# Order of emission around the block products of a ConvFFN: a norm's broadcast inside a product, weight sums a step ahead of their splits, the sample operand kept in SBUF, a second load queue

## The chip, the cores and the metric

The kernel runs on one core of one Trainium2 chip. The metric is the device time of one execution in microseconds (us). The core has a matrix engine, TensorE (PE, with a weight load, PEld, that overlaps its matmuls), VectorE (DVE), ScalarE (ACT), GpSimd (POOL) and SyncE (SP); each works its own list of instructions in order, and they wait for each other through semaphores. Transfers are issued from an engine's list (here SP's and POOL's) and carried out by the core's 16 DMA engines.

## The reference

One inference step of one layer: a mixer (retention and gated linear attention heads, with one input and one output projection), and behind it a gated ConvFFN with a causal convolution of width 3, for 1024 prompt frames and 64 sample frames of a running stream (1088 columns in all). Everything is float32. The part that the change touches is this:

```python
x = x + g1 * jnp.einsum('bte,ed->btd', mix, w_out)
h2 = _rmsnorm(x, g_norm_ffn) * (1.0 + sc2) + sh2
a, up = jnp.split(jnp.einsum('btd,df->btf', h2, w_ffn_in), 2, axis=-1)   # 1024 -> 2 x 2816
buf = jnp.concatenate([conv0.astype(a.dtype), a], axis=1)
conv = conv_b + conv_w[0] * buf[:, 0:T]
for j in range(1, CONV_W):
    conv = conv + conv_w[j] * buf[:, j:j + T]
y = jax.nn.silu(conv) * up
x = x + g2 * jnp.einsum('btf,fd->btd', y, w_ffn_out)                     # 2816 -> 1024
...
y_prompt = _rmsnorm(xp, g_final)                                         # and y_sample alike
```

The last two columns of `a` per row (`buf[:, T:]`) are outputs too (the caches).

## The kernel before

**Number format.** A float32 product is made of three passes over reduced floats: each operand is split ("cut") into a high part `hi` (a cast on ACT) and a low part `lo` (source minus `hi`, on DVE), and PE adds hi*hi, hi*lo and lo*hi. So each operand costs ACT one pass, DVE one.

**Norm ahead of the FFN (L1456, L1560 to 1608).** The output projection runs over three token groups `c` (384, 384, 320 columns) and eight row blocks `m`; each (c, m) ends with a residual addition into `hf[m]` (tiles named `ab`, or `cv` for m = 6, 7) and an addition of its squares to `sqs`. `norm2(c, sqs)` then has two halves: PE sums `sqs` over partitions (`ones`), DVE makes the reciprocal root in a dozen small operations (`na`, `nr`); PE broadcasts it over the partitions (`ident,nr`), and DVE multiplies `hf` by it and the modulation. The third group's norm is spread over the first products of FFN-in.

**FFN-in (L1488 to 1860).** The matrix product is made with seven block products p = 1..7 in place of eight (a Strassen scheme on halves of the inner dimension and halves of the columns), for 22 blocks `q` of 128 rows: 11 pairs of a convolution row and its gate row. A product is 24 matmuls of 128x272 (`product`, L1701). Its two operands are a sum or difference of weight blocks (made by `prep_in`, L1508, with its inner `need` for the sums `ws` and `raw`, and cut into a slot of three `hi` and three `lo` tiles, L1503), and a sum or difference of halves of the normed columns (`X`, made once by `operand` and `sums_b`). `prep_to(n)` has the first n products' weights made; within the loop (L1854) it runs LA = 4 products ahead. `evict_in` (L1714) takes a product out of PSUM, mostly by additions on DVE; convolution, gate and the sums of the gated rows for FFN-out's own block products (`y_sums`, L1670) are queued in `aux` and run within a budget of each step. The gated rows go to DRAM (`d_y`) from POOL's queue, the sample columns of each to `d_ys` (L1664). The first products' order (q = 0 and (1,1)) is written out by hand (L1780 to 1815).

**FFN-out (L1821 to 2246).** The list `osteps` has the steps of the seven products: "M" p=1 for 11 row blocks, "A" p=2 and p=4 in pairs of blocks, M 6, A 3, M 7, A 3, A 5 and "B" 5. For a step, weights come in through `rw` buffers (5) and gated rows through `ry` (3, M steps) or `rb` (3, A and B steps; `load_b`, L1998, and the split into `ba`, 11 buffers). All these loads are on SP's queue. A step has its operands cut three steps ahead (`prep_out`). The sample columns come back by 22 loads of 32 KB through SP (`sp_group`, L1904) and are cut into `sp`. The finished rows are added to the residual `x3` (16 loads from `d_x2`, L2141) by DVE (`add_to`); `caches` (L2102) transposes the cache rows, copies them on DVE into `cs` and stores them. Some intermediate weight sums go to DRAM (`d_e`) from POOL.

**Final norm.** `final_first` (L2084) norms the first 512 columns beside the last products. For the rest, `late_turn` transposes each 128-row group in two halves (one early, one at the end), ACT squares them with a sum (`square`), and `finish` (L2039) makes the factor and multiplies each half by it and the gain `gbc` into `yt`, with one store per group.

## Time and profile before

| | us |
|---|---|
| median of 3 runs | 1524.76 (1523.64 to 1531.74) |
| profiled execution | 1522.7 |
| its span, first to last instruction | 1520.9 |
| PE busy | 1372.5 (90%) |
| DVE busy | 1091.0 (72%) |
| ACT busy | 627.5 (41%) |
| POOL busy | 296.3 (19%) |

The mean granted clock of PE is 0.973 of full speed. The shares are means over stages with different limits, so the table by stretches further down is read first: it gives for each stretch the time that each engine was busy in it, with the number of instructions, then the granted clock, the DMA engines' share and the rate in GB/s. In a timeline a row is a run of equal instructions: its start, its time, engine, line and operation (out<-in), and in brackets how long the engine stood idle before it and who released it. L234, L239 and L91 are helpers through which most instructions go, so tiles' names tell them apart. SPq is SyncE issuing transfers.

### The profile page before, as it was taken

How to read it: one execution, taken by the hardware profiler on the slowest of the kernel's cores; microseconds unless marked ns; L12 is line 12 of the kernel's file. 1: busy time of each engine (PE TensorE's matmuls, PEld its weight loads, DVE VectorE, ACT ScalarE, POOL GpSimd, SP SyncE). 2: the span in 40 equal slices, each digit the busy share in tenths (PEclk: the TensorE clock that was granted, in tenths of full speed). 3: DMA queues.
4: the chain of work that ended last, by engine and by line, in shares of the span. 5: the costliest groups of instructions: out<-in, count | busy, mean ns of one | idle time of the engine just before them, and what ended most of it. 6: DMA issues, size and time to landing. Idle time of an engine off the chain costs nothing.

```text
span 1520.9 us, 23779 instructions
## 1 busy us (share of the span) xinstructions
PE 1372.5 (90%) x9082; PEld 1270.4 (84%) x9082; DVE 1091.0 (72%) x1992; ACT 627.5 (41%) x1253; POOL 296.3 (19%) x394
## 2 busy tenths in 40 slices
PE   5999888989989899898689999999999978899995
PEld 3778778879879898898589999999999956687874
DVE  6647878966885888667787777777777745667766
ACT  5645344432333224455454434434444433343342
POOL 3335434424332443211001111101000100000000
PEclk9999999999999999999899999999999989999998
DMA  8420101132223222564113323332233259653522
GB/s 258 151 68 15 56 19 58 42 96 85 87 87 99 77 82 68 171 196 151 33 28 106 101 85 106 106 106 63 74 105 106 97 184 334 215 164 115 178 74 111
DMA packets 165913, 165.75 MB, mean 109 GB/s; under 512 B 13289, under 2 KB 131399, under 8 KB 165799
## 3 DMA queue, kind: packets, MB, share of 16 engines
q1 hardware_dynamic: 157159, 135.99, 29.1%
q0 software_dynamic: 8640, 28.25, 4.7%
q8 instruction: 71, 1.16, 0.3%
q14 instruction: 43, 0.35, 0.1%
HBM read 130.67 MB, written 33.53 MB: 108 GB/s over the span
## 4 chain that ended last, share of the span: by engine, by line
PE 47%; DVE 27%; ACT 9%; DMA 6%; issue 6%; SPq 0%; POOL 0%; DVEq 0%; ACTq 0%; POOLq 0%
PE dX L234 17%; PE mm L234 11%; PE dA L234 6%; PE al L234 4%; PE mn L234 3%; DVE lo L91 3%; PE o L234 2%; DMA raw<-in_w_ffn_in_dram 2%; DVE ab L91 2%; ACT hi L91 2%; DVE qbd L91 2%; ACT cv L91 2%; DVE cv L91 2%; DVE acc L91 2%; DVE raw L91 2%
## 5 line engine op out<-in xcount | busy, mean ns | idle before, releaser
L234 PE MATMUL dX<-X,lo 128*128 128x272 f32 x1344 | 182.0, 291 | 15.5 <-ACT X L91 7.0
L234 PEld LDWEIGHTS dX<-X,lo 128*128 128x128 f32 x1344 | 174.3, 190 | 18.8 <-DVE ab L91 8.2
L234 PE MATMUL dX<-X,hi 128*128 128x272 f32 x1296 | 174.2, 290 | 6.3 <-DVE ab L91 5.6
L234 PEld LDWEIGHTS dX<-X,hi 128*128 128x128 f32 x1296 | 168.5, 190 | 6.7 <-issue 5.7
L234 PE MATMUL mm<-act_hi,hi 128*128 128x384 f32 (+1 forms) x480 | 169.7, 354 | 0.3 <-DVE mix L91 0.2
L234 PE MATMUL mm<-act_lo,hi 128*128 128x384 f32 (+1 forms) x480 | 158.0, 329 | 0.1
L234 PE MATMUL mm<-act_hi,lo 128*128 128x384 f32 (+1 forms) x480 | 157.7, 329 | 0.0
L91 ACT CAST hi<-raw 128x512 fp32r<-128x512 f32 (+1 forms) x122 | 97.1, 798 | 71.3 <-DVE raw L91 60.5
L234 PE MATMUL al<-ba,hi 128*128 128x512 f32 x396 | 102.2, 400 | 7.0 <-DVE x L91 7.0
L234 PE MATMUL mn<-lo,hi 128*128 128x512 f32 x396 | 99.8, 406 | 8.4 <-ACT lo L91 4.6
L234 PEld LDWEIGHTS mn<-lo,hi 128*128 128x128 f32 x396 | 76.2, 195 | 29.6 <-ACT lo L91 7.2
L91 DVE SCALAR_TENSOR_TENSOR cv<-ab,cw,cv 128x1088 f32<-128x1088 f32 x44 | 59.3, 1348 | 48.9 <-ACT cv L91 48.9
L234 PEld LDWEIGHTS mm<-act_hi,hi 128*128 128x128 f32 x480 | 91.3, 190 | 1.9 <-DVE mix L91 0.5
L234 PEld LDWEIGHTS mm<-act_lo,hi 128*128 128x128 f32 x480 | 91.2, 190 | 0.7 <-POOL act_lo L91 0.3
L234 PEld LDWEIGHTS al<-ba,hi 128*128 128x128 f32 x396 | 71.9, 191 | 22.8 <-DVE x L91 8.3
L234 PEld LDWEIGHTS mm<-act_hi,lo 128*128 128x128 f32 x480 | 90.8, 189 | 0.0
L234 PE MATMUL mm<-hi,act_hi 128*128 128x256 f32 x288 | 87.7, 304 | 0.2 <-ACT hi L91 0.2
L234 PE MATMUL mm<-lo,act_hi 128*128 128x256 f32 x288 | 82.3, 286 | 4.1 <-DVE lo L91 4.1
L234 PE MATMUL mm<-hi,act_lo 128*128 128x256 f32 x288 | 82.1, 285 | 0.0
L91 POOL TENSOR_TENSOR acc<-acc,prod 128x512 f32<-128x512 f32 x42 | 64.9, 1546 | 81.3 <-ACT prod L91 80.4
L91 DVE TENSOR_TENSOR lo<-raw,hi 128x1024 fp32r<-128x1024 f32 x49 | 64.0, 1308 | 13.7 <-ACT hi L91 13.6
L234 PE MATMUL dX<-act_hi,hi 128*128 128x384 f32 (+1 forms) x192 | 66.4, 346 | 8.0 <-DVE ab L91 7.2
(334 smaller groups left out, 3096.2 us busy)
## 6 DMA issues: line engine op xcount, KB each, us to landing
raw<-in_w_ffn_in_dram SPq DMA_DIRECT2D x44, 512.0 KB, 3.8
raw<-in_w_ada_dram SPq DMA_DIRECT2D x32, 512.0 KB, 4.0
raw<-in_w_in_dram SPq DMA_DIRECT2D x28, 512.0 KB, 3.8
raw<-in_w_out_dram SPq DMA_DIRECT2D x24, 512.0 KB, 4.0
d_y<-cv POOLq DMA_DIRECT2D x22, 512.0 KB, 4.7
rb<-d_y SPq DMA_DIRECT2D x44, 256.0 KB, 2.9
rw<-in_w_ffn_out_dram SPq DMA_DIRECT2D x41, 256.0 KB, 3.0
wa<-in_w_ada_dram SPq DMA_DIRECT2D x16, 512.0 KB, 4.9
```

Source lines behind the costliest of these rows:

```text
L91: return call(*args, **kw)
L234: T.matmul(out, lhsT, rhs, start=start, stop=stop, skip_group_check=more)
```

## The change

1. *Sample operand.* Three of the `hf` tiles (m = 3, 4, 5) move from the `ab` tiles to a pool `spp` of their own, whose three tiles are used again, once the norm is done, for the sample operand `sp` of the whole FFN. The gate writes the high half of its 64 sample columns there by an ACT copy, and DVE the low half with the next `y_sums`. `d_ys`, its 22 stores and 22 loads, and `sp_group` are gone.
2. *Entry.* The sums of q = 0 are made behind `prep_to(4)`, during the last steps of the output projection; product (0,2) is cut in two halves, with the rest of the third group's norm between; the hand order of operands, evictions and preparations is another, and the look-ahead LA is 5.
3. *FFN-out.* `rb` loads are issued by POOL; `d_e` stores go a step later; the sums of a step's weights are made a step ahead of their cut (`sum_out`); `rw` has four buffers; the PSUM tiles `mn` take other banks.
4. *Final norm.* The early halves are multiplied by the gain before the factor is known (`late_gain`), and by the factor on ACT; DVE makes the late halves alone. One small operation of the factor is gone, by a scale in the squares. The pairs of transposes in `final_first` come without a step between.

The diff, cut to its core:

```diff
-        return abp.tile([P, 2 + T2], F32, tag=tag, name=tag, bufs={"ab0": 2, "ab": 6, "cv": 2}[tag])
+        return abp.tile([P, 2 + T2], F32, tag=tag, name=tag, bufs={"ab0": 2, "ab": 3, "cv": 2}[tag])
-    hf = [ab_tile("ab" if k < 6 else "cv") for k in range(KD)]
+    hf = [ab_tile("ab" if k < 3 else "cv") if k < 3 or k > 5 else
+          spp.tile([P, T2], F32, tag="sp", name="hf", bufs=3) for k in range(KD)]
...
                 prep_to(4)
+                for n in range(1, 5):
+                    need_in(0, n)
...
-            nc.gpsimd.dma_start(out=d_ys[f], in_=cv[:, SEQ:T2])
-        aux.append(("D", fn, 1.3))
+        def hi():
+            S.copy(out=spart(f)[:, 0:SMP], in_=cvt[q // 2, n][:, SEQ:T2])
+        def lo():
+            V.tensor_tensor(out=spart(f)[:, SMP:P], in0=cvt[q // 2, n][:, SEQ:T2],
+                            in1=spart(f)[:, 0:SMP].bitcast(F32), op=ALU.subtract)
+        aux.extend([("D", fn, 1.3), ("A", hi, 0.0)])
+        small_lo.append(lo)
...
+    LA = 5
     evict_in(0, 1)
-    product(0, 2)
-    for _ in gen:
-        pass
+    prep_to(6)
+    product(0, 2, 0, 2)
+    all_of(gen)
+    product(0, 2, 2, 4)
     product(1, 1)
-    prep_to(6)
-    LA = 4
-    sums_b(1, 2 * CW - HT, HT)
-    all_of(operand(5, 0, 1 - 1, xbp))
-    sums_b(3, 2 * CW - HT, HT)
+    sums_b(1, edge, HT)
+    all_of(operand(5, 0, 0, xbp))
     product(0, 5)
     all_of(operand(3, 1, 1, xbp))
     evict_in(0, 5)
-    prep_to(8)
+    product(0, 3)
+    sums_b(3, edge, HT)
     sums_b(2, 0, HT)
-    product(0, 3)
     all_of(operand(6, 1, 1, xbp))
     evict_in(0, 3)
-    prep_to(9)
+    prep_to(7)
     product(0, 6)
     all_of(operand(7, 0, 1, xbp))
     evict_in(0, 6)
+    prep_to(8)
+    product(0, 7)
     sums_b(4, 0, HT)
-    product(0, 7)
...
-    pmn = ctx.enter_context(tc.tile_pool(name="pmn", bufs=4, space=PSUM, reuse_waits="tile"))
     pal = ctx.enter_context(tc.tile_pool(name="pal", bufs=3, space=PSUM, reuse_waits="tile"))
     psm = ctx.enter_context(tc.tile_pool(name="psm", bufs=1, space=PSUM, reuse_waits="tile"))
+    pmn = ctx.enter_context(tc.tile_pool(name="pmn", bufs=4, space=PSUM, reuse_waits="tile"))
-    ftag = {"rw": 5, "ry": 3, "rb": 3}
+    ftag = {"rw": 4, "ry": 3, "rb": 3}
-                nc.gpsimd.dma_start(out=d, in_=w)
+                stores.append((d, w))
...
-        nc.sync.dma_start(out=t, in_=d_y[i][:, YI[p]])
+        nc.gpsimd.dma_start(out=t, in_=d_y[i][:, YI[p]])
...
-    sp_group(0, 8)
-            sp_group(8, 3)
-            sp_group(11, 6)
-            sp_group(17, 5)
+        elif n + 3 < len(osteps):
+            sum_out(n + 3)
+        for d, w in late_stores:
+            nc.gpsimd.dma_start(out=d, in_=w)
+        late_stores[:] = stores
+        stores[:] = []
...
+            for j in {0: (), 1: (0,), 2: (1, 2, 3)}[n - len(osteps) + 3]:
+                late_gain(j)
...
-    for _ in finish(late, P, 4, tsq, lambda j: y_prompt[0, (4 + j) * P:(5 + j) * P, :]):
-        pass
+    rs = rsqrt(vv, 4, "n4")
+    for j in range(4):
+        r, yt = rs[:, j:j + 1], yts[j]
+        early_, (pt, cols) = cols_of(0)(yt), late[j][1]
+        S.activation(out=early_, in_=early_, func=AF.Copy, scale=r)
+        V.scalar_tensor_tensor(out=cols(yt), in0=pt, scalar=r, in1=cols(gbc), op0=ALU.mult,
+                               op1=ALU.mult)
+        nc.sync.dma_start(out=y_prompt[0, (4 + j) * P:(5 + j) * P, :], in_=yt)
```

PE at the entry to FFN-in, before: `dA<-X` and `dX<-X` are products of 24 matmuls, `ones,sqs` the sum of squares, `ident,nr` the broadcast, L239 transposes of the convolution's taps.

```order
L234 MATMUL dA<-X_7458,hi 128x272 x24
L234 MATMUL dX<-ones,sqs 128x1 x3
L239 MATMUL dX<-ident,ab_7578 128x88
L239 MATMUL dX<-ident,ab_7578 128x44
L234 MATMUL dA<-X_7515,lo 128x272 x24
L234 MATMUL dX<-ident,nr 128x128 x3
L234 MATMUL dA<-X_7458,hi 128x272 x24
L234 MATMUL dX<-X_7803,lo 128x272 x24
```

The same place on PE after the change:

```order
L234 MATMUL dA<-X_7439,hi 128x272 x24
L234 MATMUL dX<-ones,sqs 128x1 x3
L239 MATMUL dX<-ident,ab_7559 128x88
L239 MATMUL dX<-ident,ab_7559 128x44
L234 MATMUL dA<-X_7496,lo 128x272 x12
L234 MATMUL dX<-ident,nr 128x128 x3
L234 MATMUL dA<-X_7496,lo 128x272 x12
L234 MATMUL dA<-X_7439,hi 128x272 x24
```

The broadcast has moved from behind the second product to its middle.

DVE at the same place, before, from the last residual addition of the projection (`cv<-dX,G`) and around it: `raw` and `ws` are weight sums, `hi`, `lo` the low parts of cuts, `ab<-ab 128x224` and `128x320` differences of the columns; between the two halves stand the dozen small operations of the factor and the normed operands.

```order
L91 TENSOR_TENSOR lo<-ws,lo 128x512
L91 TENSOR_TENSOR ab<-ab 128x224 x6
L91 TENSOR_TENSOR ab<-cv,ab 128x224 x2
L91 SCALAR_TENSOR_TENSOR cv<-dX,G_129,cv 128x256
...
L91 SCALAR_TENSOR_TENSOR cv<-cv,A_127,dX 128x64
L91 TENSOR_TENSOR raw<-raw 128x512
L91 TENSOR_TENSOR raw<-ws,raw 128x512
L91 TENSOR_TENSOR raw<-raw 128x512
L91 TENSOR_TENSOR hi<-raw,hi 128x512
L91 TENSOR_TENSOR lo<-raw,lo 128x512
L91 TENSOR_TENSOR ab<-ab 128x320 x4
```

DVE there after the change:

```order
L91 TENSOR_TENSOR lo<-ws,lo 128x512
L91 TENSOR_TENSOR raw<-raw 128x512
L91 TENSOR_TENSOR raw<-ws,raw 128x512
L91 TENSOR_TENSOR raw<-raw 128x512
L91 TENSOR_TENSOR ab<-ab 128x224 x3
...
L91 SCALAR_TENSOR_TENSOR cv<-dX,G_129,cv 128x256
...
L91 SCALAR_TENSOR_TENSOR nr<-na,nr 128x3
L91 TENSOR_TENSOR hi<-raw,hi 128x512
L91 TENSOR_TENSOR lo<-raw,lo 128x512
L91 SCALAR_TENSOR_TENSOR ab<-ab,A_127,dX 128x256
```

The three sums stand ahead of the last residual addition, and the two subtractions of the cut ahead of the normed operands.

SP's queue at the exit of FFN-in, before, behind the last 14 sample loads (the last of them in the first row): `C` and `ry` are weights and gated rows of FFN-out, `x_...` residual rows.

```order
L1907 DMA rb<-d_ys_6486 128x64
L2136 DMA C_12847<-in_w_ffn_out_dram 128x512 x3
L1934 DMA C_12847<-in_w_ffn_out_dram 128x512
L1938 DMA ry<-d_y_6459 128x512
L2001 DMA rb<-d_y_6454 128x512
L2001 DMA rb<-d_y_6455 128x512
L2001 DMA rb<-d_y_6456 128x512
L2108 DMA out_dram<-cs 44x128
L2141 DMA x_0_0_12849<-d_x_6453 128x512
```

The same place on SP after the change:

```order
L1946 DMA C_12852<-in_w_ffn_out_dram 128x512
L1950 DMA ry<-d_y_6458 128x512
L2159 DMA C_12852<-in_w_ffn_out_dram 128x512 x3
L1946 DMA C_12852<-in_w_ffn_out_dram 128x512
L1950 DMA ry<-d_y_6459 128x512
L2125 DMA out_dram<-cs 44x128
L2164 DMA x_0_0_12854<-d_x_6453 128x512
```

The sample loads and the `rb` loads have left SP's queue; the `rb` loads stand on POOL's, behind its last store of `d_y`, and later between the `d_e` stores.

## Rows read from the trace of the kernel before

**Rows 1.** Table by stretches; columns in its first row (x: instructions; PEclk: granted clock).
```profile
core 0: us, PE busy (x) PEld busy (x) DVE busy (x) ACT busy (x) POOL busy (x), PEclk, DMA share, GB/s
705.00:776.00 71.00, 47.71 (x287) 45.30 (x287) 57.22 (x118) 36.06 (x75) 4.78 (x12) 0.83 0.14 43
776.00:1216.00 440.00, 433.99 (x3443) 431.79 (x3442) 324.53 (x440) 187.40 (x313) 38.99 (x120) 1.00 0.29 93
1225.20:1282.20 57.00, 42.73 (x158) 31.19 (x158) 25.52 (x41) 18.73 (x33) 3.46 (x7) 0.88 0.85 286
1282.20:1319.60 37.40, 36.89 (x179) 28.94 (x178) 24.04 (x39) 11.29 (x20) 5.93 (x11) 1.00 0.67 223
...
1396.00:1504.50 108.50, 105.85 (x478) 85.06 (x479) 76.96 (x143) 41.15 (x83) 0.00 (x0) 1.00 0.38 124
1504.50:1520.90 16.40, 2.56 (x20) 1.85 (x18) 8.96 (x23) 3.11 (x10) 0.00 (x0) 0.67 0.32 128
```

**Rows 2.** Waits of PE, 705 to 776; total, times, longest.
```profile
PE dX L234 <- ACT X L91: 7.0, 1, 7.0
```

**Rows 3.** Timeline of PE at the entry; start, time, run of instructions.
```profile
731.97 4.72 PE L234 MATMUL dA<-X,lo 128*128 128x272 f32 x24 [0.94 <-ACT ab L91]
...
778.99 3.17 PE L234 MATMUL dX<-X,lo 128*128 128x272 f32 x24
```

**Rows 4.** Timeline of DVE at the entry.
```profile
737.40 3.59 DVE L91 SCALAR_TENSOR_TENSOR ab<-ab,A,dX 128x256 f32<-128x256 f32 x12 [4.50 <-PE dX L234]
...
742.07 0.69 DVE L91 TENSOR_TENSOR raw<-raw 128x512 f32<-128x512 f32 x1
...
746.10 1.69 DVE L91 TENSOR_TENSOR ab<-ab 128x320 f32<-128x320 f32 x4
```

**Rows 5.** Waits of PE, 790 to 1216, the products.
```profile
PE dX L234 <- DVE ab L91: 6.0, 10, 1.5
```

**Rows 6.** Timeline of SP's queue at the exit; L1907 sample loads, L2141 residual loads.
```profile
1226.82 13.47 SPq L1907 DMA_DIRECT2D rb<-d_ys  x14
...
1250.79 1.75 SPq L2141 DMA_DIRECT2D x<-d_x  x4
```

**Rows 7.** Timeline of PE at the exit.
```profile
1238.10 1.22 PE L234 MATMUL sm<-hi,sp 128*128 128x512 f32 x2 [7.74 <-DVE sp L91]
1239.12 5.09 PE L234 MATMUL mn<-lo,hi 128*128 128x512 f32 x12
...
1244.53 3.01 PE L234 MATMUL mn<-lo,hi 128*128 128x512 f32 x12
```

**Rows 8.** Transfers of the stretch 1255 to 1282: packets, bytes, mean rate.
```profile
DMA packets 6583, 9.75 MB, mean 361 GB/s; under 512 B 1612, under 2 KB 2533, under 8 KB 6581
```

**Rows 9.** Timeline of POOL at the exit: its last store of FFN-in.
```profile
1232.26 0.54 POOL L1687 DMA_DIRECT2D d_y<-ab  x1
```

**Rows 10.** Transfers issued 1282 to 1320: count, KB each, median us to landing.
```profile
rb<-d_y SPq DMA_DIRECT2D x9, 256.0 KB, 4.9
d_e<-rw POOLq DMA_DIRECT2D x9, 256.0 KB, 3.4
```

**Rows 11.** Timeline of PE between the A steps of p=2 and p=4.
```profile
1325.54 1.65 PE L234 MATMUL al<-ba,hi 128*128 128x512 f32 x3 [5.96 <-DVE x L91]
```

**Rows 12.** Timeline of DVE there.
```profile
1324.74 1.40 DVE L91 SCALAR_TENSOR_TENSOR x<-al,G,x 128x512 f32<-128x512 f32 x2
```

**Rows 13.** Tile rb: idle time of its engines before it; us, times.
```profile
  DMA rb<-d_y: 20.3, 13
```

**Rows 14.** Timeline of PE in the last products; L239 transposes rows.
```profile
1498.00 0.66 PE L239 MATMUL al<-ident,x 128*128 128x128 f32 x4 [1.74 <-DVE yt L91]
```

**Rows 15.** Tile yt: least/median/most ns, first to last start; DMA landing.
```profile
L2052 SPq DMA_DIRECT2D out_dram<-yt x9: 332/333/511, 1393.3 to 1517.0; - x9
...
L91 DVE SCALAR_TENSOR_TENSOR yt<-mn,n4r,gbc x4: 741/741/742, 1512.1 to 1516.2; 128x512 f32<-128x512 f32 x4
...
DMA to landing us min/median/max: 2.6/2.6/2.6
```

More of the change, by code (lines that the diff above doesn't have):

```diff
@@ L1378, in stream_step_kernel @@
     d_y = [scr.tile([P, 7, 512], F32, name=f"d_y{i}") for i in range(KF)]
-    d_ys = [scr.tile([P, SMP], F32, name=f"d_ys{f}") for f in range(NF)]
     d_e = {}
@@ L1506, in combo_slot, with need_in @@
         return wp.tile(shape, F32R, tag=tag, name=tag, bufs=3)
+    def need_in(q, n):
+        if (q, n) in sums:
+            return 0.0
+        (a11, a12), (a21, a22) = ((raws[q, i][:, 0:4], raws[q, i][:, 4:8]) for i in range(2))
+        cost = 0.7
+        if n == 1:
+            s = sums[q, 1] = fw.tile([P, 4, P], F32, tag="ws", name="ws", bufs=2)
+            plus(s, a21, a22)
+            return cost
+        if n == 3:
+            cost += need_in(q, 1)
+            sub(a21, a11, a21)
+        elif n == 2:
+            cost += need_in(q, 3)
+            sub(a11, sums[q, 1], a11)
+        else:
+            cost += need_in(q, 2)
+            sub(a12, a12, a11)
+        sums[q, n] = True
+        return cost
     def prep_in(q, p):
@@ L1699, in run_aux, with product @@
                 last_d[0] = now[0]
-    def product(q, p):
+    def product(q, p, k0=0, k1=4):
         grp = {1: "A", 2: "A", 6: "B", 7: "B", 5: "C", 3: "C", 4: "D"}[p]
         first = p in (1, 6, 5, 4)
-        if first:
+        if first and k0 == 0:
             held[q, grp] = pair("dA" if grp == "A" else "dX")
         o = held[q, grp]
-        t, x = combos.pop((q, p)), X[p]
-        for k in range(4):
+        t, x = combos[q, p], X[p]
+        for k in range(k0, k1):
             for a, b in ((0, 0), (0, 1), (1, 0)):
@@ L1778, in cached_taps, with all_of @@
         plus(e01[:, 0], e01[:, 0], et)
+    def all_of(g):
+        for _ in g:
+            pass
+    LA = 5
+    edge = 2 * CW - HT
     gen = norm2(2, sqs)
@@ L1953, in load_to, with sum_out @@
             o_load[0] += 1
+    def sum_out(n):
+        st = osteps[n]
+        kind, p = st[:2]
+        if kind == "M" and p == 6:
+            w = rw[n] = ft("rw")
+            sub(w, C2[:, st[2]], C1[:, st[2]])
+        elif kind == "M" and p == 7:
+            sub(rw[n], C1[:, st[2]], rw[n])
+        elif kind == "A" and p == 3:
+            u, i, k = st[2:]
+            w = rw[n][:, 0:k]
+            sub(w, w, C2[:, i:i + k, u * 256:u * 256 + 256])
+    stores = []
     def prep_out(n):
```

95 lines of the change are left out of this document (38 added, 57 removed).

## Prediction

> **What bounds the kernel now.** I read the table by stretches first [rows 1]: for each stretch of the span it has TensorE's (PE) busy time, the granted clock and the DMA engines' share. The change touches nothing before 705 us (the mixer and the first two token groups of the norm), so only later stretches count. They are limited by different things. From 776 to 1216 us, the block products of FFN-in, PE is busy 433.99 of 440.00 us at a clock of 1.00: only 6 us are there to be had. The entry to that stretch (705 to 776) has PE busy 47.71 of 71.00, with DVE (VectorE) busy 57.22: DVE holds it up. The exit (1225.2 to 1282.2) has PE busy 42.73 of 57.00 and the DMA share at 0.85: transfers hold it up. From 1396 to 1504.5 PE is busy again (105.85 of 108.50), and the tail of 16.40 us is DVE and the last stores. So the change can win in the gaps: about 23 us at the entry, 6 in the products, 14 at the exit, 6 at one stall, 3 in the last products, and part of the 16 of the tail.
>
> **The change part by part.** The sums below are made against the profiled execution, 1522.7 us (span 1520.9); the median of the runs stands 2.1 us above it.
>
> *Entry.* The chain of waits here: PE runs product (0,2) whole, 4.72 us from 731.97, and broadcasts the norm factors only behind it [rows 3]. DVE, which had the factors ready, waits 4.50 us for that broadcast, makes the normed operands (737.40 on), then three weight sums and a pair of splits (742.07 to 746.10, 4.0 us), and only then the differences that feed operand 5, for which PE waits 7.0 us [rows 2, 4]. The change cuts product (0,2) in two halves with the broadcast between them, so the broadcast comes 12 matmuls (half of 4.72, so about 2.4 us) earlier; and it puts the three sums ahead of the norm's last residual add and the splits' two subtractions just before the normed operands. The sums (3 x 0.72 = 2.2 us) therefore lie on the path to the statistics and push them back 2.2; the earlier broadcast gives 2.4 back. So the normed operands start where they did, and the 4.0 us behind them are gone from the path. Against this, the look-ahead of 5 puts one more sum and one more split (0.69 each, 1.4 us) into DVE's queue ahead of an eviction, and the sums for operands 3 and 2 now stand behind product (0,3) in the program, which PE reaches sooner than DVE finishes them. I keep half of the 4.0: -2. Ends: -5 (the 4.0 whole, and 1 of the 3.0 that is then left of the 7.0) and +2.2 (nothing but the delay).
>
> *Products, 776 to 1216.* PE's only waits of size are 6.0 us in 10 pieces, on evictions by DVE [rows 5]: each is the eviction of a block's last product, queued behind the next weights' sums. With a look-ahead of 5 those sums are made one product (3.17 us, [rows 3]) earlier, in front of another eviction. Since the longest piece is 1.5, less than a product, most should vanish; but with all six operand slots in use a split can now wait for the product before it to end. Bounds: -6 (all ten gone), and +7 (each of ten blocks loses one 0.69 split on the path). I take -4, since DVE is busy only 324.53 of 440.00 here and has room. The sample part costs nothing here: 22 copies on ACT (187.40 of 440.00 busy) and 22 subtractions of 64 columns on DVE, under 0.4 us each by the 128x512 row of 0.69, some 8 us of DVE time in 115 us of idle time; POOL loses 22 stores. If that cover were gone the cost would be those 8 us.
>
> *Exit.* SP is held 13.47 us issuing 14 of the 22 sample loads, since the last wait for samples that the final gate has only just stored [rows 6]. Behind it stand the loads of FFN-out's weights and products, the `rb` loads, the cache store and the 16 residual loads `x3`, which begin at 1250.79. PE waits 7.74 us for the split of the first sample group (and before that for the last eviction, whose banks it needs); its next step then runs 5.09 us instead of the 3.01 that the same step takes at 1244.53 [rows 7]. After that the stretch is bound by transfers: 361 GB/s at a share of 1.04 [rows 8]. The change takes the 22 loads, their splits and both PE waits away. What is late next: the `x3` loads. They stand on SP behind the cache store, which waits for a DVE copy, which stands behind the first `ba` split, which waits for the first `rb` load. That load is now on POOL's queue behind the last `d_y` store (1232.26, 0.54 us to issue [rows 9]), so it goes out at about 1233, lands 4.9 later by [rows 10], and `x3` begins at about 1240 or 1241 instead of 1250.79. The same bytes follow at the same rate, so the end of the stretch moves by about as much: -10. Ends: -13 (the 13.47 whole) and -5 (transfers were already partly under way in the wait, and only the PE waits' half is won).
>
> *The stall at 1319.6.* PE is still for 5.96 us between the A steps of p=2 and of p=4 [rows 11]. The chain: the `x` additions of DVE (1.40 us for two [rows 12]) that free the PSUM banks stand behind `ba` splits, and those wait for `rb` loads (20.3 us in 13 waits over the whole kernel [rows 13]), which take 4.9 us to land there [rows 10] on a queue where the `rw` loads are issued in between, each behind its own buffer. With a queue of their own the `rb` loads go out as soon as their buffer is read. What is left is the two additions: 5.96 - 1.40, about -4.5. Ends: -8 (the whole wait, and the 2.1 us that a step lost after the wait of 7.74, by 5.09 against 3.01 in [rows 7], if the matmuls behind this one lose as much) and 0 (the loads' landing, not their issue, is what is late).
>
> *Middle stages.* One `rw` buffer fewer, sums a step ahead and stores of `d_e` a step later: PE has little idle there, so 0, ends 0 and +3 (one wait of 3.4 us, the landing of a `d_e` store [rows 10], should a buffer come free late).
>
> *Last products.* The transposes of the early rows wait 1.74 us for the `yt` passes of the pair before [rows 14]; now they are done in pairs, earlier, and the sums stand a step ahead of their splits. -1.7, ends -3 (all of the 2.65 idle) and +2 (eight transposes in a row wait for the residual additions).
>
> *Tail.* Eight `yt` passes on DVE stand behind the norm factor, the second at 1512.1 and the eighth at 1516.2, so 0.69 us apart; a store of 512 KB leaves after each pair, the last at 1517.0, and lands in 2.6 [rows 15]. Four passes become four gains made early by DVE and four scalings by ACT beside the rest: 4 x 0.69 = 2.8 less of passes. But the four stores, 2 MB, then leave 0.69 apart instead of 1.4, and 2 MB at the 361 GB/s of [rows 8] take 5.8 us, more than the 4.2 us (1512.1 + 0.74 to 1517.0) over which they left. If that rate binds, the first store is earlier by one pass (0.7) and nothing else is won. I take -1.3, between the two but nearer to the rate's; ends -3 and -0.6.
>
> Sum: -2 - 4 - 10 - 4.5 + 0 - 1.7 - 1.3 = -23.5. So 1522.7 - 23.5 = 1499.2 for a profiled execution, and **1500** for a median of runs, with about 1 of the 2.1 us that it stood above.
>
> **A rule against it.** `rb` loads and SP's loads overlap already in the trace, at a share of 1.04 for 27 us [rows 8]: there, a second queue has no idle engine to fill. The Trainium skill ("DMA: Bandwidth & Descriptors", section "Issuing engines are not separate DMA queues") says that transfers started from several engines run on the same 16 DMA engines, and that this saves only the time to start them. By that rule the stall would stay whole and the exit would win only what the sample loads held; that is the first rival.
>
> **The rivals.** (1) *The second queue brings nothing.* `rb` loads land as late as before, since the engines are full: the stall term is 0, and the first `rb` load, behind stores and full engines, lets `x3` begin only at about 1245: exit -5. The sum is -2 - 4 - 5 - 1.7 - 1.3 = -14, so 1509. For it speaks the share of 1.04; against it that it is 0.67 from 1282 to 1319 [rows 1], where the `rb` loads are late. (2) *The order at the entry and the look-ahead bring nothing*: +2.2 and 0 instead of -6, so -23.5 + 8.2 = -15.3: 1507 to 1508. It decides if DVE reaches the statistics later than PE the middle of product (0,2). (3) *Slower: POOL's loads land late.* All A steps eat three `rb` buffers in a ring; 33 loads follow the first 11, so a landing of L instead of 4.9 us costs 33 x (L - 4.9) / 3 = 11 x (L - 4.9). The rest of the change gains 19, so it decides at L = 6.6, and L = 8 gives +34 - 19: about 1538. For it: [rows 10] show a 256 KB transfer through POOL's queue only as a store. Against it: that store lands in 3.4 us, less than SP's loads. The Trainium skill (same page, section "SWDGE vs HWDGE vs iDMA") has POOL's descriptors written by software, which DVE can lock out of SBUF in some modes; 0.54 us to issue, with DVE busy, shows no such hold here.
>
> **How the numbers follow.** Forecast 0.62, its own range 1489 to 1509; rival 1 0.19; rival 2 0.10; rival 3 0.06; anything else 0.03. The range for 8 in 10 reaches down to 1486 (entry, products, exit and stall at their better ends are 11.5 below the sum, the tail's 1.7 more) and up to 1513, over both rivals of the gaining side. Half a per cent, 7.6 us, is about what a measurement of this kernel can tell from no change. Faster than that means under 1517: the forecast and rivals 1 and 2, less a little for a mix of their worse ends, 0.88; within it 0.06; slower 0.06.
>
> **What would show it.** After the change, PE should wait less than 3 us for the third operand at the entry and reach its first regular block products about 2 us sooner; the waits on `ab` in the products should fall from 6.0 to about 2; no wait of PE on the sample operand should be left, SP free at 1226, `x3` begin some 15 us after that; p=2 start at about 46 instead of 57 us after the exit begins; the stall be under 2 us; and only four `yt` passes stand behind the norm factor. The prediction is wrong if the `rb` loads from POOL take over 6.6 us to land, if the `x3` loads still begin some 25 us after the exit begins, or if PE's waits in the products grow instead of shrinking.

## The result, and the profile after

The changed kernel takes 1505.89 us (median of 4 runs, 1502.89 to 1508.56) against 1525.57 for the kernel before, timed beside it: a ratio of 0.9864, 95% interval 0.9829 to 0.9899, so 19.7 us less. The forecast was 1500 with a range of 1486 to 1513, faster with a chance of 0.88. The profiled execution took 1507.2 us with a span of 1505.4 (1522.7 and 1520.9 before).

The sum was right to 6 us, but its terms were not. To see that, both spans are cut at the same events of PE: the projection's last transposes, the first regular product into `dA`, the end of FFN-in's last product, the first A step of p=2, the first of p=4, the first M step of p=6, the first A step of p=3, the first B step, the last transposes, the end.

| stretch | before | after | difference | forecast |
|---|---|---|---|---|
| up to the projection's last transposes | 720.05 | 723.05 | +3.0 | 0 |
| entry | 61.95 | 61.73 | -0.2 | -2 |
| block products of FFN-in | 443.21 | 434.94 | -8.3 | -4 |
| exit (M steps of p=1) | 56.81 | 48.03 | -8.8 | -10 |
| p=2 and the stall behind it | 43.52 | 45.58 | +2.1 | -4.5 |
| p=4 | 42.88 | 43.93 | +1.1 | 0 |
| M steps of p=6, A steps of p=3 | 35.69 | 32.67 | -3.0 | 0 |
| M 7, A 3, A 5 | 61.33 | 60.75 | -0.6 | 0 |
| B steps | 39.27 | 39.70 | +0.4 | -1.7 |
| tail | 16.19 | 15.02 | -1.2 | -1.3 |

The first line is not the change's: up to there the same kernels and their variants below took from 716.6 to 724.2 us, in no order. Without it the profiled executions differ by 18.5 us. The table by stretches of the changed kernel, in its own cuts, answers [rows 1]:

```profile
core 0: us, PE busy (x) PEld busy (x) DVE busy (x) ACT busy (x) POOL busy (x), PEclk, DMA share, GB/s
784.78:1219.72 434.94, 434.37 (x3459) 434.15 (x3458) 323.67 (x450) 191.20 (x335) 28.62 (x100) 1.00 0.29 94
1219.72:1267.75 48.03, 40.28 (x157) 28.82 (x157) 23.75 (x40) 16.79 (x31) 8.82 (x17) 0.96 0.91 311
1267.75:1313.33 45.58, 37.07 (x181) 29.13 (x179) 29.15 (x47) 16.34 (x29) 12.73 (x24) 0.95 0.63 207
1313.33:1357.26 43.93, 43.43 (x218) 35.71 (x219) 28.16 (x48) 16.67 (x31) 5.04 (x10) 0.93 0.53 173
1357.26:1389.93 32.67, 32.67 (x158) 27.37 (x157) 27.14 (x59) 14.24 (x28) 1.64 (x3) 1.00 0.45 140
```

In the products PE now has 0.6 us of idle time in 434.94, and in the M and A steps of p=6 and 3 none. What is left stands at the exit (7.8 us), at the stall (8.5) and at the entry.

**Entry.** PE's waits there, answering [rows 2] (from 705 to 790: total, times, longest):

```profile
PE dX L234 <- DVE sqs L91: 6.6, 1, 6.6
PE dX L234 <- DVE ab L91: 5.5, 2, 2.8
...
PE dX L234 <- ACT hi L91: 1.4, 1, 1.4
PE dX L234 <- ACT X L91: 1.3, 1, 1.3
```

The 7.0 us for `X` are 1.3 now. The timeline of PE, answering [rows 3], and of DVE's wait for the broadcast, answering [rows 4]:

```profile
734.15 1.41 PE L234 MATMUL dX<-ones,sqs 128*128 128x1 f32 x6 [6.63 <-DVE sqs L91]
...
763.58 5.78 PE L234 MATMUL dX<-X,hi 128*128 128x272 f32 x24 [2.73 <-DVE ab L91]
...
774.03 3.52 PE L234 MATMUL dX<-X,hi 128*128 128x272 f32 x24 [1.43 <-ACT hi L91]
780.33 4.61 PE L234 MATMUL dX<-X,lo 128*128 128x272 f32 x24 [2.79 <-DVE ab L91]
784.78 3.16 PE L234 MATMUL dA<-X,hi 128*128 128x272 f32 x24
```

```profile
741.41 1.84 DVE L91 SCALAR_TENSOR_TENSOR ab<-ab,A,dX 128x256 f32<-128x256 f32 x6 [2.29 <-PE dX L234]
```

DVE's wait for the broadcast went from 4.50 to 2.29 us, as worked out (2.4 less). Product (0,7) starts 40.5 us after the projection's last transposes (763.58 - 723.05); before it was 47.5 (767.53 - 720.05). So 7 us were won, and all but 0.2 given back from there to the first regular product, 21.2 us where it was 14.5: by waits of 1.43 and 2.79 us that were not there before and by slower products.

**Exit.** SP's queue, answering [rows 6], and POOL's, answering [rows 9] (`rb` loads are L2019):

```profile
1220.01 0.38 SPq L1950 DMA_DIRECT2D ry<-d_y  x1
1234.85 0.33 SPq L2125 DMA_DIRECT2D out_dram<-cs  x1
1235.23 1.75 SPq L2164 DMA_DIRECT2D x<-d_x  x4
```

```profile
1227.09 0.54 POOL L1702 DMA_DIRECT2D d_y<-ab  x1
1227.63 1.63 POOL L2019 DMA_DIRECT2D rb<-d_y  x3
```

SP is free of the sample loads, and the residual loads begin 15.5 us after the exit's start (25.6 before). But SP then stands still for 14.5 us, from 1220.4 to 1234.85, at the cache store, exactly behind the chain that the prediction named as what is late next: `rb` loads behind POOL's last stores.

**Stall.** PE between p=2 and p=4, answering [rows 11], the landings, answering [rows 10], and ACT in the same place:

```profile
1313.33 1.65 PE L234 MATMUL al<-ba,hi 128*128 128x512 f32 x3 [8.02 <-DVE x L91]
```

```profile
rb<-d_y POOLq DMA_DIRECT2D x9, 256.0 KB, 3.8
```

```profile
1308.86 0.62 ACT L91 CAST lo<-rw 128x512 fp32r<-128x512 f32 x1 [3.06 <-DMA rw<-in_w_ffn_out_dram]
```

The stall grew from 5.96 to 8.02: within it ACT, whose casts DVE needs, now waits 3.06 us for an `rw` load. Before, it waited there for `rb` loads:

```profile
1318.97 1.28 ACT L91 CAST ba<-rb 128x512 fp32r<-128x512 f32 x2 [2.16 <-DMA rb<-d_y]
```

The median landing of `rb` loads, 3.8 against the 4.9 of [rows 10], does not show that they come sooner: e2_rb_sp below says why.

### The profile page after: what moved, and what is told of

Read it like the earlier page. It is cut to its first block, busy times and chain, and to the rows that moved or that the text cites. A ratio compares the mean times of both kernels' runs of the same rounds, so it can differ in the third digit from the quotient of the medians.

```text
span 1505.4 us, 23828 instructions
## 1 busy us (share of the span) xinstructions
PE 1374.1 (91%) x9082; PEld 1275.0 (85%) x9082; DVE 1088.3 (72%) x2006; ACT 631.0 (42%) x1275; POOL 309.2 (21%) x416
## 4 chain that ended last, share of the span: by engine, by line
PE 57%; DVE 23%; issue 6%; ACT 5%; DMA 4%; POOL 1%; SPq 0%; DVEq 0%; ACTq 0%; POOLq 0%
PE dX L234 25%; PE mm L234 10%; PE dA L234 8%; PE al L234 4%; PE mn L234 3%; PE o L234 3%; DVE qbd L91 2%; DVE lo L91 2%; DVE att L91 2%; DVE acc L91 2%; ACT hi L91 1%; DVE X L91 1%; DMA rb<-d_y 1%; DVE ab L91 1%; PE sc L234 1%
## 5 line engine op out<-in xcount | busy, mean ns | idle before, releaser
L234 PE MATMUL mn<-lo,hi 128*128 128x512 f32 x396 | 96.5, 398 | 7.8 <-ACT lo L91 6.1
```

The lines of the kernel that those rows point to most:

```text
L234: T.matmul(out, lhsT, rhs, start=start, stop=stop, skip_group_check=more)
```

## The experiments

The stretches of every run, in us, from its own profile. The last line is from the projection's last transposes to the end, so it leaves the mixer's spread out. e6_la4, e7_sum_now, e9_sums_after and e10_unsplit were executed once each. The others were timed beside the kernel before, on three chips, where it took 1527.1 us (e1 to e4), 1523.7 (e5 and e8) and 1525.3 (e11), so their ratios compare better than their medians.

| stretch | before | after | e1_rw5 | e2_rb_sp | e3_rb_mix | e4_la45 | e5_adds_first | e6_la4 | e7_sum_now | e9_sums_after | e10_unsplit | e8_best | e11_best2 |
|---|---|---|---|---|---|---|---|---|---|---|---|---|---|
| entry | 61.95 | 61.73 | 61.69 | 62.87 | 61.68 | 59.88 | 60.43 | 59.92 | 60.40 | 57.95 | 62.36 | 58.36 | 56.52 |
| products | 443.21 | 434.94 | 434.95 | 435.21 | 434.94 | 435.44 | 435.47 | 443.18 | 435.50 | 435.47 | 435.48 | 436.79 | 436.26 |
| exit | 56.81 | 48.03 | 47.40 | 42.27 | 42.69 | 47.74 | 47.57 | 47.87 | 47.82 | 47.64 | 48.12 | 42.01 | 42.34 |
| p=2, stall | 43.52 | 45.58 | 42.68 | 45.81 | 46.58 | 45.53 | 39.64 | 46.43 | 46.88 | 45.34 | 46.45 | 39.32 | 39.50 |
| p=4 | 42.88 | 43.93 | 43.96 | 42.60 | 42.73 | 43.26 | 47.18 | 43.91 | 43.86 | 42.73 | 42.95 | 41.27 | 42.79 |
| M 6, A 3 | 35.69 | 32.67 | 32.67 | 32.68 | 32.67 | 32.91 | 33.20 | 32.71 | 37.06 | 32.67 | 32.67 | 32.69 | 32.69 |
| M 7, A 3, A 5 | 61.33 | 60.75 | 60.75 | 60.75 | 60.75 | 60.75 | 60.75 | 60.75 | 61.95 | 60.75 | 60.75 | 60.75 | 60.75 |
| B steps | 39.27 | 39.70 | 40.16 | 38.55 | 43.50 | 39.69 | 39.52 | 39.63 | 42.04 | 39.74 | 39.52 | 39.02 | 39.00 |
| tail | 16.19 | 15.02 | 15.42 | 15.28 | 14.83 | 15.04 | 15.05 | 15.05 | 15.04 | 15.04 | 15.06 | 15.65 | 15.70 |
| from the transposes | 800.85 | 782.35 | 779.68 | 776.02 | 780.37 | 780.24 | 778.81 | 789.45 | 790.55 | 777.33 | 783.36 | 765.86 | 765.55 |

A stretch that a run's edit does not touch moves between runs too: the entry from 60.4 to 62.9 us, p=2 from 45.3 to 46.5, p=4 from 42.7 to 43.9, the others by less than 1. In p=4 it is the granted clock: for the same matmuls PE is busy 43.43 us at 0.93 in the changed kernel, and in e8_best

```profile
1297.02:1338.29 41.27, 40.77 (x217) 33.53 (x218) 31.29 (x53) 19.68 (x37) 0.00 (x0) 1.00 0.63 199
```

Differences inside these are not read by the times; there the waits must tell.

**e1_rw5: the buffer of `rw` given back.**

```diff
-    ftag = {"rw": 4, "ry": 3, "rb": 3}
+    ftag = {"rw": 5, "ry": 3, "rb": 3}
-        junk = fo.tile([P, 512], mybir.dt.bfloat16, tag="junk", name="junk", bufs=2)
+        junk = fo.tile([P, 512], mybir.dt.bfloat16, tag="junk", name="junk", bufs=1)
```

> The changed kernel with five rw buffers again (one buffer of the squares' scrap tile given up for the room). In the changed kernel PE stands still 8.02 us between the A steps of p=2 and p=4, and ACT waits 3.06 and 1.36 us there for rw loads, not for rb loads. Theory A (the buffer taken from rw is what holds the stall): ACT's waits on rw loads go, the stall falls to 2 to 4 us, the stretch from the first A step of p=2 to the first of p=4 from 45.6 to about 41, the whole time by about 5 us. Theory B (the stores of the weight sums a step later, or the transfer rate, make the loads late): the stall stays at 7 to 8 us and the time within 1 us.

Median 1504.45 us, ratio 0.9852 (0.9834 to 0.9870). PE's waits from the first A step of p=2 to the end of p=4:

```profile
PE al L234 <- DVE x L91: 6.1, 3, 5.1
```

The stall, the longest of the three, is 5.1 us instead of 8.0, the stretch 2.9 shorter, and ACT's two waits for `rw` loads ahead of the additions are gone. ACT waits for `rb` loads there, as it did before the change:

```profile
1303.38 0.62 ACT L91 CAST ba<-rb 128x512 fp32r<-128x512 f32 x1 [1.71 <-DMA rb<-d_y]
```

(The changed kernel has such a wait too, of 1.93 us; the expectation overlooked it.) So the buffer explains that the stall grew, but not the stall: theory A in half its size. At 5.1 it is about where it was before the change, although `rb` loads have a queue of their own.

**e2_rb_sp: the second load queue undone.**

```diff
-        nc.gpsimd.dma_start(out=t, in_=d_y[i][:, YI[p]])
+        nc.sync.dma_start(out=t, in_=d_y[i][:, YI[p]])
```

> The changed kernel with the rb loads back on SP's queue, all else kept: the second load queue alone undone. Theory A (the second queue is worth something, as the prediction had it): the stall before p=4 grows from 8 to 10 us or more and the time by 2 to 5 us; at the exit nothing changes. Theory B (the second queue costs at the exit: POOL issues the first rb loads only behind its last stores of the gated rows, at 1227.6, and the cache copy and the 16 residual loads wait for them until 1235.2): with SP issuing them early, the residual loads begin 5 to 8 us sooner, the exit stretch of 48.0 us falls to 41 to 45, and the time by up to 5 us, less what the stall grows by.

Median 1498.88 us, ratio 0.9811 (0.9785 to 0.9837), so about 7 us better than the changed kernel, though the two intervals still touch (0.9829 to 0.9837). SP's queue at the exit, which in this run starts at 1222.3:

```profile
1223.03 2.22 SPq L2019 DMA_DIRECT2D rb<-d_y  x3
...
1232.10 2.76 SPq L2164 DMA_DIRECT2D x<-d_x  x4
```

The first `rb` loads go out 0.8 us after the exit starts instead of 7.9, the residual loads 9.8 us after it instead of 15.5, and the exit is 5.8 us shorter: theory B. At the stall nothing is lost: the stretch is 45.81 against 45.58. The landings of tile `rb` in this run,

```profile
DMA to landing us min/median/max: 2.8/4.9/8.0
```

against 2.9/3.7/6.9 from POOL, look later, but the trace has a landing for only 5 of the 44 loads from SP, and for all 44 from POOL. (In the kernel before it is 4 of 44, and the 4.9 of [rows 10] is one load.) What the trace has more of are ACT's casts that waited for such a load: they began 3.2 us (median of 20) after the issue on SP and 3.4 us (of 19) after the issue on POOL. Near the stall, on SP:

```profile
1300.00 0.89 SPq L2019 DMA_DIRECT2D rb<-d_y  x2
1303.32 1.23 ACT L91 CAST ba<-rb 128x512 fp32r<-128x512 f32 x2 [3.15 <-DMA rb<-d_y]
```

So neither queue is shown to be the quicker. In the B steps the loads from SP do better: 38.6 to 39.0 us with them on SP (e2, e8, e11), 39.5 to 40.2 with them on POOL (seven runs; e3 mixes the two, and e7 moves the sums).

The rule of the Trainium skill that the prediction weighed ("DMA: Bandwidth & Descriptors", section "Issuing engines are not separate DMA queues") holds for the stall. What was dearer here: a second queue puts the loads behind whatever stands in it.

**e3_rb_mix: the first three loads on SP, the rest on POOL.**

```diff
-        nc.gpsimd.dma_start(out=t, in_=d_y[i][:, YI[p]])
+        (nc.sync if b_load[0] < 3 else nc.gpsimd).dma_start(out=t, in_=d_y[i][:, YI[p]])
```

> The changed kernel with the first three rb loads issued by SP and all later ones by POOL. Theory A (as in the run with all rb loads on SP: the first loads behind POOL's stores hold the cache copy and the residual loads): residual loads begin at about 1228 instead of 1235.2, the exit stretch falls from 48.0 to 41 to 45 us and the stall stays at 8: the time falls by 3 to 6 us. Theory B (the exit is bound by the bytes that have to move, share 0.91): the residual loads begin sooner, but the stretch stays within 1 us of 48.0.

Median 1504.39 us, ratio 0.9855 (0.9836 to 0.9874). The exit is 5.3 us shorter, theory A again. But the B steps take 3.8 us more, which no theory had. POOL and ACT ahead of them:

```profile
1436.47 1.63 POOL L2019 DMA_DIRECT2D rb<-d_y  x3 [79.18 <-DVE ba L91]
```

```profile
1439.55 0.62 ACT L91 CAST ba<-rb 128x512 fp32r<-128x512 f32 x1 [4.58 <-DMA rb<-d_y]
```

In the changed kernel two of these three loads go out as soon as two buffers are read, the third later; here all three wait for the third buffer's split. That the mix of two queues on one ring of buffers makes the waits coarser is an inference from this one place.

**e4_la45: a look-ahead of 4 at first.**

```diff
-        cost = prep_to(s + 1 + LA)
+        cost = prep_to(s + 1 + (LA if s >= 14 else 4))
```

> The changed kernel with a look-ahead of 4 in the first seven steps of the loop and 5 from then on. In the changed kernel the entry is up to 7 us ahead at product (0,7) and gives it back in waits of 1.43 and 2.79 us at the next products. Theory A (the look-ahead of 5 puts an additional preparation ahead of the eviction of (0,4) while DVE has no idle time): the wait of 2.79 shrinks by about 1.4 us or goes, the entry (last transposes of the projection to the first regular dA product, 61.7 us) becomes 58 to 60, products stay at 434.9, time -2 to -3. Theory B (DVE is simply full at the entry, whatever the order): the wait moves to a later product, entry and products together stay within 0.7 us of 496.6.

Median 1505.95 us, ratio 0.9860 (0.9829 to 0.9890): no difference that the times show. In the profile the entry is 1.9 us shorter, which is little outside its spread, and the products 0.5 longer. PE at the place of the two waits:

```profile
774.55 5.81 PE L234 MATMUL dX<-X,hi 128*128 128x272 f32 x24 [2.84 <-ACT hi L91]
780.16 3.44 PE L234 MATMUL dX<-X,lo 128*128 128x272 f32 x24
```

The wait of 2.79 is gone, and that of 1.43 has become 2.84. DVE ahead of the addition that the wait of 2.79 was for (`ab<-ab,dX`), in the changed kernel, where the sum and the split of one more preparation stand before it:

```profile
777.42 0.68 DVE L91 TENSOR_TENSOR raw<-raw 128x512 f32<-128x512 f32 x1
778.86 0.69 DVE L91 TENSOR_TENSOR hi<-raw,hi 128x512 fp32r<-128x512 f32 x1 [0.76 <-ACT hi L91]
779.47 0.71 DVE L91 TENSOR_TENSOR ab<-ab,dX 128x544 f32<-128x544 f32 x1
```

and in e4, where that sum and that split come behind it:

```profile
777.95 0.72 DVE L91 TENSOR_TENSOR ab<-ab,dX 128x544 f32<-128x544 f32 x1
```

Counted from the start of product (0,7), that is 15.9 and 13.9 us: the look-ahead holds this addition back 2.0 us, so theory A has the cause. In all eight runs with a look-ahead of 5 (the changed kernel, e1, e2, e3, e5, e7, e9, e10) the product behind it starts 16.8 us after product (0,7), however long PE waited for it (0.5 to 2.8 us); with 4 at first (e4, e6, e8, e11) it starts after 14.7 to 16.1. What the times gain is less: entry and products together are 1.4 us shorter than in the changed kernel, since 0.5 comes back in the products. Theory B has that part: DVE is busy 15.72 of 15.76 us between 747.74 and 763.50 in the changed kernel, and what is taken from one place of a full engine can show up at another.

**e5_adds_first: the additions ahead of the splits.** In the last A step of p=2 the block of preparations is issued behind the additions into the residual (the block itself is unchanged; the loop that makes sure of a step's own `ba` tiles now stands ahead of it, and in the traces DVE's order behind FFN-in differs in nothing but the place of the two additions):

```diff
+        behind = kind == "A" and p == 2 and st[2] == 1 and st[3] + st[4] == KF
+        if not behind:
+            ahead()
...
                 if p == 3 and u:
                     first_final = flow.start(final_first(), 1.0)
+            if behind:
+                ahead()
```

> The changed kernel, with one difference: in the last A step of p=2 the two additions into the residual (and the copy of the sample sum) are issued ahead of that step's splits and sums for later steps, not behind them. It asks what ends the stall of 8.02 us. Theory A (DVE's order: PE needs the two additions, 1.40 us, and they stand behind splits that wait for rw and rb loads): the additions follow the last matmul of p=2 and one split, the stall falls to about 2.5 to 3 us, the stretch p=2 to p=4 from 45.6 to about 40.5; the time by 4 to 5 us. Theory B (the loads set the pace, whoever waits for them): the stall splits up, PE waits at the next steps of p=4 for ba or for the weights, and p=2 to M6 together stay within 1 us of 89.5.

Median 1499.76 us, ratio 0.9844 (0.9822 to 0.9866). PE at the stall and later in p=4, and ACT in p=4:

```profile
1299.70 0.95 PE L234 MATMUL al<-ba,hi 128*128 128x512 f32 x3 [2.09 <-DVE x L91]
...
1325.46 1.65 PE L234 MATMUL al<-ba,hi 128*128 128x512 f32 x3 [2.58 <-DVE x L91]
```

```profile
1313.05 0.62 ACT L91 CAST lo<-rw 128x512 fp32r<-128x512 f32 x1 [4.58 <-DMA rw<-in_w_ffn_out_dram]
...
1320.39 0.62 ACT L91 CAST lo<-rw 128x512 fp32r<-128x512 f32 x1 [5.59 <-DMA rw<-in_w_ffn_out_dram]
```

Both theories are half right. The stall is 2.1 us and its stretch 5.9 shorter, so DVE's order ends it; but 3.3 us come back inside p=4, where by ACT's waits of 4.58 and 5.59 us the `rw` loads are late, with four buffers and two loads for each step. Of the two stretches together 2.7 us are won.

**e6_la4: the look-ahead alone undone.**

```diff
-    LA = 5
+    LA = 4
```

> The changed kernel with a look-ahead of 4, as before the change. Theory A (the look-ahead is what took PE's waits on evictions out of the block products): these waits come back to about 6 us in some 10 pieces, the products from 434.9 to about 442 us, and the entry from 61.7 to about 60. Theory B (the waits went because DVE and POOL were relieved of the sample stores and y sums were reordered, or because of the other order at the entry): they stay under 2 us and the products within 1.5 us of 434.9.

One execution: 1511.69 us. The products take 443.18 us, the 443.21 of before, and PE's waits from 790 to 1216 are back:

```profile
PE dX L234 <- DVE ab L91: 5.0, 9, 1.4
```

In the changed kernel that row reads 0.6 in one piece. So the look-ahead carries the whole term, 8.2 us. That is more than the waits alone, since the product behind a wait is slower as well:

```profile
876.01 3.30 PE L234 MATMUL dX<-X,lo 128*128 128x272 f32 x24 [1.40 <-DVE ab L91]
879.15 3.17 PE L234 MATMUL dA<-X,hi 128*128 128x272 f32 x24
```

**e7_sum_now: weight sums where they are split.**

```diff
-            sum_out(3)
-        elif n + 3 < len(osteps):
-            sum_out(n + 3)
...
     def prep_out(n):
         kind, p = st[:2]
+        sum_out(n)
```

> The changed kernel with each weight sum of FFN-out made where its split is made, as before the change, not a step ahead. The stretch from the first M step of p=6 to the first A step of p=3 took 35.69 us before and takes 32.67 now; the prediction had nothing for it. Theory A (the sum and its split stand in a row, DVE, ACT, DVE, and the split's low part came late for PE, 0.8 and 0.3 us at a time): the stretch goes back to 35 to 36. Theory B (it was the transfers: rb and rw loads no longer behind each other): it stays within 0.7 us of 32.67.

One execution: 1513.58 us. The stretch goes from 32.67 to 37.06, the next from 60.75 to 61.95 and the B steps from 39.70 to 42.04: theory A, and 7.9 us in the three together (8.2 from the transposes to the end). PE's waits in the first of them, where the changed kernel has none:

```profile
PE mn L234 <- ACT lo L91: 1.1, 2, 0.8
PE mn L234 <- DVE lo L91: 0.8, 3, 0.3
```

Why the stretch is 1.4 us longer than in the kernel before (35.69), with nearly the same waits (1.9 against 1.8 us), is open.

**e9_sums_after: the early sums of q = 0 behind the last addition of squares.**

```diff
                 prep_to(4)
-                for n in range(1, 5):
-                    need_in(0, n)
...
+    for n in range(1, 5):
+        need_in(0, n)
     gen = norm2(2, sqs)
     product(0, 1)
```

> The changed kernel with the three early weight sums of q = 0 (and one already made) moved behind the last addition of squares, so that they lie in DVE's wait for PE's sum of squares and not on the path to it. In the changed kernel PE waits 6.63 us for that addition (4.61 before the change). Theory A (the three sums, 2.1 us, are what delayed the statistics, and PE's next operands follow from these): the wait falls to about 4.6 us, the reciprocal starts 1.5 us sooner, the entry from 61.7 to about 60.2. Theory B (DVE is full through the whole entry, so its total work sets the end and not the order): the wait falls, but the entry stays within 0.5 us of 61.7.

One execution: 1501.31 us. PE's wait is back at 4.58 us, and the entry falls by 3.8 us, more than theory A had:

```profile
731.22 1.03 PE L234 MATMUL dX<-ones,sqs 128*128 128x1 f32 x6 [4.58 <-DVE sqs L91]
```

Product (0,7) starts 2.4 us sooner: 38.1 us after the transposes, against 40.5 or 40.6 in the changed kernel and in e1 to e8, all nine. That is theory A. The other 1.3 us are in the last product before the first regular one, which starts 16.8 us after product (0,7) in both. Here, and in e7, whose edit lies behind FFN-in:

```profile
777.03 3.26 PE L234 MATMUL dX<-X,lo 128*128 128x272 f32 x24 [2.79 <-DVE ab L91]
```

```profile
778.55 3.26 PE L234 MATMUL dX<-X,lo 128*128 128x272 f32 x24 [0.50 <-DVE ab L91]
```

In the changed kernel the same product takes 4.61 us (780.33, above): the granted clock is at its lower level from 780.0 to 783.4 there, and at the upper one throughout in e9. The changed kernel, e1, e2, e3, e5 and e7 run the same order of instructions up to FFN-out, and yet this product takes 3.1 us up to the first regular one in e5 and e7, 4.4 in e1, e3 and the changed kernel, and 5.6 in e2. So these 1.3 us are not shown to be the edit's.

**e10_unsplit: product (0,2) whole.**

```diff
-    product(0, 2, 0, 2)
-    all_of(gen)
-    product(0, 2, 2, 4)
+    product(0, 2)
+    all_of(gen)
```

> The changed kernel with product (0,2) whole and the broadcast of the norm factors behind it, as before the change: the split of the product alone undone. Theory A (the prediction: the broadcast is 12 matmuls earlier, and DVE waits for it): DVE's wait for the broadcast grows from 2.29 to about 4.5 us and the entry from 61.7 to 63.5 to 64. Theory B (DVE has enough other work, or PE is given the time back later): the entry stays within 0.5 us of 61.7.

One execution: 1508.69 us. DVE's wait for the broadcast:

```profile
743.88 1.84 DVE L91 SCALAR_TENSOR_TENSOR ab<-ab,A,dX 128x256 f32<-128x256 f32 x6 [4.24 <-PE dX L234]
```

It grows from 2.29 to 4.24 us as theory A had it, and product (0,7) starts 42.5 us after the transposes, 2.0 later than in the nine runs above. The entry as a whole is only 0.6 us longer (62.36), inside the spread of the untouched, because the last product before the first regular one takes 3.1 us here and 4.4 in the changed kernel, as it does in runs that do not touch the entry. So theory A holds as far as product (0,7), and the entry as a whole does not decide.

**e8_best and e11_best2: what the runs point to.** e8_best is the changed kernel with the edits of e1, e2, e4 and e5; e11_best2 has that of e9 as well.

> The changed kernel with four things together: rb loads on SP's queue, five rw buffers, a look-ahead of 4 in the first seven steps of the loop, and the two additions ahead of the splits in the last A step of p=2. If the single effects add up: exit 42.3 us instead of 48.0, p=2 to p=4 about 40.5 instead of 45.6, entry 59.9 instead of 61.7, so 11 to 13 us less than the changed kernel's 782.4 us from the projection's last transposes to the end, and a median of about 1492 to 1495. If the last two of FFN-out do not add up (SP's loads in one queue again, which the additions no longer wait for but the next steps do), the median is 1496 to 1499, as with the queue alone.

Median 1489.06 us, ratio to the kernel before 0.9766 (0.9747 to 0.9785). The effects more than add up: from the transposes to the end it takes 16.5 us less than the changed kernel, where 11 to 13 were expected (exit 42.0, p=2 39.3, p=4 41.3, entry 58.4; the products are 1.9 longer). Its waits of PE through p=2 and p=4, where the changed kernel has 9.0 us, of which 8.0 in one piece:

```profile
PE al L234 <- DVE x L91: 2.8, 3, 1.8
```

With five buffers and the loads on SP the cost of e5 inside p=4 is gone (41.27 against 47.18).

> The best kernel so far (rb loads on SP, five rw buffers, look-ahead of 4 at first, the two additions first; median 1489.1) with the early weight sums behind the last addition of squares. If the sums' place is worth 1.5 us at the entry, the entry goes from 58.4 to 57 us and the median to about 1487 to 1488; if DVE's total work sets the end there, it stays at 58.4 and 1489.

Median 1485.89 us (6 runs, 1483.60 to 1490.02), ratio 0.9750 (0.9722 to 0.9778): the fastest here, though its interval overlaps that of e8_best. Product (0,7) starts 38.2 us after the transposes (40.6 in e8_best), as in e9, and the entry is 1.8 us shorter; p=4 is 1.5 longer, at a granted clock of 0.96 and not 1.00, so the two profiles end 0.3 us apart.

## Why the prediction was right, and where not

The direction and the size held, and so did the mechanism of the products and of most of the exit; the total is 5.9 us above the forecast, inside the range. The stall's mechanism did not hold, and that the total came so near is in part luck: terms that came out 12.9 us worse than forecast (the stall alone 6.6) stand against others 7.9 better, of which 3.6 were forecast as nothing. By its own steps:

- **Entry, -2, measured -0.2.** Its two sides were right: the early sums push the statistics back 2.0 us (PE's wait on `sqs` 4.61 to 6.63, worked out 2.2) and product (0,7) 2.4 (e9); the half product gives DVE 2.2 back and product (0,7) 2.0 (e10). That product starts 7.0 us sooner for it and for the 4.0 taken off the path. What was mis-sized is what stands behind it, 6.7 us longer than before. The look-ahead, put at 1.4 us, has 2.0 of them (e4), since its split also waits 0.76 us for ACT. Some 1.4 are the granted clock in the last product, by chance as far as the runs show (e9). The other 3.3 are waits of PE for what DVE and ACT make no sooner than before; no run takes the new order there apart.
- **Products, -4, measured -8.3.** The mechanism was right and e6 shows it alone. The size was half: the prediction read "only 6 us are there to be had" off PE's busy time. All of the 6.9 us of waits in the whole stretch but 0.6 went, not two thirds, and the product behind a wait, which was 0.12 us slower (e6), counted as busy. The feared price of a full set of operand slots is not in the profile.
- **Exit, -10, measured -8.8.** Right in its number, but by two parts that e2 separates: the rest of the change, the sample loads and the wait for the last eviction above all, is worth 14.5 us (56.81 to 42.27), more than the better end of -13, which counted SP's 13.47 alone and not PE's 2.16 for the bank of the last eviction; and the second queue takes 5.8 of it back, by its first three loads (e3). The prediction saw that the first `rb` load would stand behind POOL's stores, and when; it didn't set this against the same load on SP.
- **Stall, -4.5, measured +2.1.** The step that failed is "with a queue of their own the `rb` loads go out as soon as their buffer is read. What is left is the two additions". A queue of their own does not help: the additions stand behind whatever DVE was given before them, be it a split that waits for `rb` or one that waits for `rw`. e5 shows the order as the cause (8.02 to 2.09 us), e1 that the lost buffer cost 2.9 us, e2 that with four `rw` buffers the queue is worth nothing here.
- **Middle stages, 0, measured +1.1, -3.0 and -0.6.** The +1.1 is PE at a granted clock of 0.93 in p=4, where it was 0.96: 43.43 us busy, and 42.38 before. The prediction priced the sums a step ahead at nothing. e7 puts them at 7.9 us over M 6 to the end of the B steps. The rows of PE's short waits for `lo` were not looked for there, since PE seemed busy.
- **Last products, -1.7, measured +0.4.** The wait of 1.74 us on `yt` [rows 14] is gone; in its place transposes wait 1.62 us for the additions, which the step had as its other end, and PE's wait for a split grew from 0.7 to 1.2 us. With the `rb` loads on SP (e2) the wait of 1.62 is 0.4, and the term would be -0.7: the second queue cost it about 1 us.
- **Tail, -1.3, measured -1.2.** Four passes of DVE remain where eight stood, and they save 2.8 us; the stores, closer together, then take 5.7 us from the last issue to the end where they took 3.9. The rows that answer [rows 15]:

```profile
L91 ACT ACTIVATE yt<-yt,n4r x4: 705/706/721, 1496.9 to 1498.7; 128x512 f32<-128x512 f32 x4
L91 DVE SCALAR_TENSOR_TENSOR yt<-mn,n4r,gbc x4: 743/743/752, 1496.9 to 1498.9; 128x512 f32<-128x512 f32 x4
L2294 SPq DMA_DIRECT2D out_dram<-yt x4: 332/333/917, 1497.8 to 1499.7; - x4
```

Of the rivals, the first (the second queue brings nothing) was right on the stall and wrong on the exit only because other parts won more there; its time, 1509, is 3 us off, the forecast's 6. The second's half on the entry came true in that nothing was won there, its half on the look-ahead did not. The third, late landings through POOL, did not come true: their median is 3.7 us, under its 6.6. The 4.9 us for SP that this rival and the exit reckon with is the landing of one load. And the issue at 1232.26, read as one "with DVE busy", fell where DVE stood idle, from 1231.2 to 1237.35; the 44 issues after the change, 0.55 us each with DVE busy in much of the time, are what shows no hold.

What stays open: why the stretch M 6 to A 3 in e7 is longer than in the kernel before, and what the sample operand is worth without the change of banks, which was not tried alone.

## What to carry to other kernels

Before moving loads to another engine's queue, list what stands in that queue ahead of the first of them, and who waits for that first one: here it cost 5.8 us at one place and gave nothing at the other. A wait that ends with "DVE x" is ended by DVE's order as much as by the work: look at what DVE was given before the operation that PE needs, and give it that first. And when a buffer is taken from a ring to make room, price it in the stage that uses two buffers in a step.

## What the runs showed of the hardware

A 256 KB load issued by POOL landed in 3.7 us (median of 44, 2.9 to 6.9), and POOL spent 0.55 us on each issue; SP spent 0.34 (median of the same 44 loads in e2_rb_sp). That loads from POOL land sooner or later than from SP is not shown: the trace has only five of SP's landings.

The granted clock is not the same in every execution of the same instructions: in the 20 to 22 us behind product (0,7) it was 0.77, 0.78, 0.86, 0.92, 0.91 and 0.75 in the changed kernel, e1, e2, e3, e5 and e7, and 1.00 (the upper level, 2.4 GHz, throughout) in e9. In e9 and in the changed kernel:

```profile
760.20:780.12 19.92, 13.15 (x97) 12.38 (x97) 17.89 (x33) 8.71 (x14) 1.85 (x4) 1.00 0.20 58
```

```profile
763.50:784.78 21.28, 16.99 (x96) 16.42 (x97) 19.25 (x35) 8.70 (x14) 1.85 (x4) 0.77 0.24 71
```

PE was busy 13.15 and 16.99 us, but only 1.3 us of these 3.8 reached the time, since DVE set the start of the last product, 16.8 us after product (0,7), at every clock. What made the clock fall (to 1.2 GHz) in the one and not in the other is not shown: PE's wait at the start of the entry was 6.6 or 6.7 us in all six.
